# A hybrid attention and linear-attention encoder layer: the pace at which side work is dealt out between the matmuls of the projections

## Chip, cores and metric

The kernel runs on one core of one Trainium2 chip. The metric is the time of one execution on the device in microseconds (us); lower is better. Engines are named as in the profile: PE (TensorE matmuls), PEld (its weight loads), DVE (VectorE), ACT (ScalarE), POOL (GpSimd) and SP (SyncE, which here only issues DMAs).

## What is computed

One encoder layer over 512 tokens of width 2048, in float32:

```
h = rmsnorm(x, attn_norm_w); proj = h @ w_in
aq, ak, av, gq, gk, gv, gr, glr = split(proj)
attn = mixture_of_dilations(aq, ak, av, rel_bias_table)    # 16 heads x 64, softmax over a banded, biased score matrix
log_a = log_sigmoid(glr @ gla_gate_w + gla_gate_b) / 16    # one for each direction
o = gla(gq, gk, gv, log_a_fwd) + flipped gla(..., log_a_bwd)   # 4 heads, dk 128, dv 256, a gated linear recurrence
gla_out = rmsnorm_per_head(o) * gla_norm_w * silu(gr)
x = x + concat(attn, gla_out) @ w_out
h = rmsnorm(x, ffn_norm_w)
x = x + (silu(h @ w_gate) * (h @ w_up)) @ w_down           # hidden width 5632
out = rmsnorm(x, final_norm_w)
```

## The kernel before

Each float32 operand of a large product is split into a rounded part ("hi", made by ACT) and a rest ("lo", made by DVE as operand minus hi), and a product is three matmuls: hi·hi, hi·lo, lo·hi (lines 337 to 339 and 346 to 348). Nearly all the time is a long row of such matmuls. The order of instructions on every engine is written out by hand; each engine runs its own list in that order and waits on semaphores.

**Jobs and halves.** `run_job` (from line 305) runs one block of 512 output columns. A job has 16 (or 8) "halves"; one half is one 128-row slice of the weights, multiplied into four PSUM banks, three matmuls of 512 columns to a bank. The order of the jobs that matter here is: q and k of linear attention for two heads (gqk0), its v (gv0), then gqk1 and gv1, 16 halves each; then the first halves of three column blocks of `w_out`, which need only attention's result (o1, o2, o3: 8 halves each); column block 0 of `w_out` whole (out0: 16 halves); the rest of blocks 1 to 3 (c1, c2, c3: 8 halves each); then gate and up (`ff.run`) and down. Weights come by `st.load` (an SP DMA, line 209), are rounded some halves ahead (ACT, line 237) and get their rest from DVE (line 218).

**Side work.** Attention and linear attention are Python generators whose turns are dealt out between matmuls by credit. For jobs with `fine = True` (gqk0 to gv1 and o1 to o3) a quarter of the job's `rate` is credited after each bank, and a whole credit buys one turn; after the last bank of a half as many turns as there are whole credits. For out0 to c3 the whole rate is credited once for each half. The rates are `RATES = (2.5, 5.0)`: 2.5 turns to a half in gqk0 to gv1, 5.0 in o1 to o3; out0 to c3 have 1.0. The queue `side` holds first the low-rank gate input (14 turns), then `attention()` (70 units of two turns), then, from the end of gv0, `turns(... gla(h) ..., APART)` over the four heads of linear attention. `turns` begins a head every 12 rounds and gives a round two turns: one for each of two heads at work, or one real and one empty turn where only one is.

A unit of attention goes through scores (PE, 631 and 632), maximum (DVE, 641), exponential (ACT, 649), reciprocal and, for odd units, scaling (DVE 652, ACT 658), transposes (PE, 663), rounding (ACT, 671), rest (DVE, 677) and the product with v (PE, 687 and 688), each a turn or two after the one before. A head of linear attention has 22 stages, among them the gate input (PE 924, ACT 934 to 936, DVE 937), prefix sums (DVE 946, 952), centring (DVE 964 to 967), exponentials (ACT 974 to 976), products (DVE 983), the masked score blocks and transposes (PE 1015 and 1018, DVE 1021, ACT 1025), state sums (PE 1040, ACT 1049), the chain of states (DVE 1059), the output product (PE 1087), its norm, and transposes (PE 1111, DVE 1114).

**Other queues.** `urgent` is a second queue; `run_urgent` gives its first generator one turn. It is called at the start of every `run_side`, and by `before_out` at the start of each half of c1 to c3. It carries `load_qk` (operands of the next pair of heads), `gates()` (silu of the output gate times linear attention's output, then hi and lo of that: the operands of halves 8 to 15 of out0) and `rest()` of each output block (squares, transposes, and the operands of gate and up). `gates()` is queued at the norm stage of the last head. A third generator, `ff.ahead()` (DVE additions at line 1478), sums blocks of gate weights in advance; `j.ahead` of its turns are credited for each half. It has 21 blocks of four additions and needs 85 turns.

`before_out(c)` also loads the first gate and up blocks by `ff.load` (SP, line 1390), forms their sums by `ff.sums` (DVE, 1409 to 1411, twice a call) and splits them by `ff.split` (ACT 1422, DVE 1427). It counts halves through c2 and c3: `i` is 0 to 7 in c2, 8 to 15 in c3.

**Banks and slots.** The eight PSUM banks, and the tiles ("slots") in two pools, are handed out first freed, first used. At the end of a job its four banks are emptied by DVE (836, 839 after gqk; 1297 after o1 to c3) or ACT (862 after gv).

Of the kernel before, what the change touches and what calls it, by code (L numbers as in the profile page):

```python
# [26 lines left out]
KT = D // P  # L27
# [85 lines left out]
def put(*slots):  # L113
    for s in slots:
        if s.home is not None:
            s.home.free.append(s.i)


def layer(nc, tc, x, attn_norm_w, w_in, rel_table, gw_f, gb_f, gw_b, gb_b, gla_norm_w, w_out,
# [7 lines left out]
    with tc.manual_schedule(), \  # L127
# [118 lines left out]
        def piece512(w, col, kt):  # L246

            ws = w if isinstance(w, list) else [(w, col)]
            n = 512 // len(ws)
            segs = []  # L250
            for i, (wi, c) in enumerate(ws):
                src = wi[kt * P:(kt + 2) * P, c:c + n].rearrange("(k p) c -> p k c", p=P)
                segs.append((src, lambda t, i=i, n=n: t.rearrange("p (k c) -> p k c", k=2)[:, :, i * n:(i + 1) * n]))
            return segs
# [9 lines left out]
        def run_urgent():  # L264
            while urgent:
                try:
                    next(urgent[0])
                    break
                except StopIteration:
                    urgent.popleft()  # L270
# [26 lines left out]
        def job(kind, pieces, kts, acts, evac, rate=0.0, before=None, start=None, limit=None):  # L297

            j = Job()
            j.kind, j.kts, j.acts, j.evac, j.rate, j.before, j.start, j.limit = \  # L300
                kind, kts, acts, evac, rate, before, start, limit
            j.first = len(st.halves)
            st.add(pieces)
            j.n = len(st.halves) - j.first
            jobs.append(j)
            return j
# [63 lines left out]
        def rstd_of(*a):  # L370
            for _ in rstd_parts(*a):
                pass
# [15 lines left out]
        def rows_of(rstd):  # L388

            b = ps.get()  # L390
            for t in range(4):
                mm(b.t[:, t * P:(t + 1) * P], rstd[:, t:t + 1].to_broadcast([P, P]), idn,
                   start=True, stop=True)
            s = s2.get()
            act.copy(s.t, b.t)
            put(b)
            return s

        def weighted(tiles, k, wc, f):

            b = ps.get()
            for t in range(4):
                pe.transpose(b.t[:, t * P:(t + 1) * P], tiles[t].t[:, (k % 4) * P:(k % 4 + 1) * P], idn)
            act.activation(f, b.t, AF.Copy, scale=wcol[:, wc + k:wc + k + 1])
            put(b)
# [106 lines left out]
        def squares(c, t, tiles, ss, at_=None):  # L512
            junk = s2.get()
            m = c + (4 * t if at_ is None else at_)
            act.activation(junk.t, tiles[t].t, AF.Square, accum_out=ss[:, m:m + 1])
            put(junk)
# [314 lines left out]
        def evac_gqk(pr):  # L831
            def f(banks):
                for i in range(4):
                    t = s2.get()
                    if i < 2:
                        dve.scalar_tensor_tensor(t.t, banks[i].t, P ** -0.5, rb[1].t,
                                                 op0=OP.mult, op1=OP.mult)
                    else:
                        dve.tensor_tensor(t.t, banks[i].t, rb[1].t, op=OP.mult)
                    put(banks[i])  # L840
                    pool.dma_start(out=gqd[4 * pr + i], in_=t.t)
                    put(t)
            return f
# [13 lines left out]
        def evac_gv(pr):  # L857
            def f(banks):
                for t in range(4):
                    if t % 2 == 0:  # L860
                        v = s4.get(F32, [P, 2, 512])
                    act.activation(v.t[:, t % 2], banks[t].t, AF.Copy, scale=rstd1[:, t:t + 1])
                    put(banks[t])
                    if t % 2:
                        pool.dma_start(out=gvd[2 * pr + t // 2], in_=v.t.rearrange("p b c -> p (b c)"))
                        put(v)
                if pr == 0:
                    side.append(turns(deque(gla(h) for h in range(NG)), APART))
            return f
# [349 lines left out]
                fr.late()  # L1219

        n_front = len(jobs)
        RATES = (2.5, 5.0)
        APART = 12
        for pr in range(2):
            seg = [(w_in, C_GQ + pr * 256), (w_in, C_GK + pr * 256)]
            job("A", [piece512(seg, None, k) for k in range(0, KT, 2)], list(range(KT)), acts_h,
                evac_gqk(pr), rate=RATES[0], start=gstart if pr == 0 else None,
                before=None if pr else before_first, limit=3)
            job("B", [piece512(w_in, C_GV + pr * 512, k) for k in range(0, KT, 2)], list(range(KT)), acts_h,
                evac_gv(pr), rate=RATES[0])  # L1230

# [4 lines left out]
        def free_h():  # L1236
            for k in range(KT):
                put(*hT.pop(k))
            put(rb.pop(1))
# [54 lines left out]
        def evac_out(c, part=False):  # L1294
            def f(banks):
                for t in range(4):
                    dve.tensor_tensor(x1[c][t].t, x1[c][t].t, banks[t].t, op=OP.add)
                    put(banks[t])
                if not part:
                    urgent.append(rest())  # L1300

            def rest():
                yield
                for t in range(4):
                    squares(c, t, x1[c], ss2)
                    pool.dma_start(out=xd[4 * c + t], in_=x1[c][t].t)
                if c == 3:
                    dve.tensor_reduce(sum2, ss2.rearrange("p (t c) -> p t c", c=4), op=OP.add,
                                      axis=mybir.AxisListType.X)
                    rstd_of(sum2, 4, rstd2, 1.0 / D, scr)  # L1310
                fs_ = {}
                for q in (2 * c, 2 * c + 1):
                    fs_[q] = s4.get(F32, [P, 2, 512])
                    for k in range(2):
                        weighted(x1[c], 2 * q + k, W_FFN, fs_[q].t[:, k])
                    yield
                put(*x1.pop(c))
                if c == 3:
                    rb[2] = rows_of(rstd2)
                for q in (2 * c, 2 * c + 1):  # L1320
                    yield from pair_operands(q, fs_.pop(q))
            return f

        def before_out(c):
            def f(i):
                run_urgent()
                if c >= 2:
                    i += 8 * (c - 2)
                    if i >= 6:
                        ff.most = 3 if i < 9 else 5  # L1330
                        ff.load()
                    if i in (8, 9, 11, 12, 14):
                        ff.sums(ff.n_sums, halves=True)
                    if i in (13, 15):
                        ff.split((i - 13) // 2)
            return f

        def start_out(c):
            def f():
                if c == 1:  # L1340
                    free_h()
                if c == 3:
                    load_gates()
                load_res(c)
            return f

        def drop_mix(k):
            put(*mixh.pop(k))

        def job_out(c, a, z, evac, **kw):  # L1350
            return job("B", [piece512(w_out, c * 512, k) for k in range(a, z, 2)], list(range(a, z)),
                       lambda k: mixh[k], evac, limit=3, **kw)

        for c in (1, 2, 3):
            job_out(c, 0, 8, evac_out(c, True), rate=RATES[1], start=start_out(c))
        n_in = len(jobs)
        for j in jobs[n_front:]:
            j.fine = True
        jobs[n_front + 3].lead = lambda i: AHEAD + (i > 11) + (i > 13)
        j = job_out(0, 0, KT, evac_out(0), rate=1.0, start=start_out(0))  # L1360
        j.drop = lambda k: drop_mix(k) if k < 8 else None
        for j in jobs[n_front + 4:]:
            j.lead = lambda i: AHEAD + 2
        for c in (1, 2, 3):
            j = job_out(c, 8, KT, evac_out(c), rate=1.0, before=before_out(c))
        j.drop = drop_mix

        n_out = len(jobs) - 1
# [650 lines left out]
        for c in range(4):  # L2019
            j = job("B", [piece512(w_down, c * 512, k) for k in (0, 2)], list(range(4)),  # L2020
                    lambda k: gT[k], evac_down(c), before=before_down(c))
# [6 lines left out]
        for c in range(4):  # L2028
            j = job("B", [piece512(w_down, c * 512, k) for k in (LAST - 4, LAST - 2)], list(range(LAST - 4, LAST)),
                    lambda k: gT[k], evac_later(c), before=before_later(c))  # L2030
# [96 lines left out]
        run_last = finish()  # L2127
        state["sums"] = ff.ahead()
        for n, j in enumerate(jobs):
            j.ahead = 2.0 if n_in <= n < n_out else 1.0 if n_in - 3 <= n < n_in else 0.0  # L2130
        for n, j in enumerate(jobs):
            if n == n_down:
                dn.run()
# [40 lines left out]
```

## Time and profile before

| | |
|---|---|
| time, median of 3 runs | 2173.07 us (2172.14 to 2173.58) |
| the profiled execution | 2172.39 us, span 2170.6 us |
| PE, PEld, DVE, ACT busy | 99%, 87%, 84%, 56% |
| matmuls | 12682 |
| bytes moved | 405.71 MB, 187 GB/s |
| granted TensorE clock | 0.999 |

The profile names an instruction by engine, line, and output and input tile. "Idle before" is the time that an engine waited just before an instruction, with what ended the wait. A matmul's row lasts longer than the matmul holds PE, since matmuls are pipelined: the distance from one start to the next is what it costs.

### The profile page before, as it was taken

The numbers are of one execution on the slowest core, as the hardware profiler recorded it, in microseconds if no ns is written. First come the engines' busy times: TensorE is split into PE (matmuls) and PEld (weight loads), VectorE is DVE, ScalarE is ACT, GpSimd is POOL, SyncE is SP. The second block draws the span as 40 slices with busy tenths as digits, with TensorE's granted clock in tenths as the row PEclk, the third lists the DMA queues.
The fourth block names the chain that finished last, engine by engine and source line by source line (L and its number), as shares of the span: only waits on it lengthen the run. The fifth ranks groups of instructions, "written<-read, shape, count | busy, mean of one in ns | idle before, by whom it ended". The sixth has DMA issues, their size and how long they took to land.

```text
span 2170.6 us, 34926 instructions
## 1 busy us (share of the span) xinstructions
PE 2151.7 (99%) x12682; PEld 1898.7 (87%) x12682; DVE 1824.4 (84%) x3161; ACT 1221.2 (56%) x2228; POOL 358.0 (16%) x499
## 2 busy tenths in 40 slices
PE   9999999999999999999999999999999999999998
PEld 7888887888877888888888888888888899999987
DVE  6689996777778769899899898998989888898885
ACT  8455555677655546455555555555555655555562
POOL 0012213111021110021221112211221120021300
PEclk9999999999999999999999999999999999999999
DMA  6467779445365684477766677676776985576982
GB/s 202 138 177 183 178 183 250 151 139 174 123 224 175 235 278 137 136 182 182 187 178 182 181 180 196 173 184 178 177 199 176 267 205 174 180 182 156 289 304 78
DMA packets 264411, 405.71 MB, mean 187 GB/s; under 512 B 19309, under 2 KB 163357, under 8 KB 264238
## 3 DMA queue, kind: packets, MB, share of 16 engines
q1 hardware_dynamic: 205502, 272.49, 39.3%
q0 software_dynamic: 58416, 130.45, 26.4%
q8 instruction: 100, 1.64, 0.3%
q14 instruction: 73, 0.60, 0.1%
q10 hardware_dynamic: 320, 0.53, 0.1%
HBM read 287.47 MB, written 66.39 MB: 163 GB/s over the span
## 4 chain that ended last, share of the span: by engine, by line
PE 58%; DVE 0%; DMA 0%; issue 0%; ACT 0%; DVEq 0%; ACTq 0%
PE ps L1518 24%; PE ps L1504 12%; PE ps L1877 5%; PE ps L1876 5%; PE ps L1875 5%; PE ps L347 1%; PE ps L346 1%; PE ps L348 1%; PE ps L2072 1%; PE ps L2070 1%; PE ps L2071 1%; DMA gd<-b 0%; DVE b L1427 0%; DVE a L2103 0%; DVE a L1538 0%
## 5 line engine op out<-in xcount | busy, mean ns | idle before, releaser
L1422 ACT CAST b<-b 128x768 fp32r<-128x768 f32 (+1 forms) x569 | 518.9, 944 | 370.4 <-DVE b L1427 172.8
L1427 DVE TENSOR_TENSOR b<-b,b 128x768 fp32r<-128x768 f32 (+1 forms) x569 | 597.0, 1084 | 29.8 <-ACT b L1422 18.5
L1518 PE MATMUL ps<-b,b 128*128 128x512 f32 x1656 | 484.1, 393 | 0.4 <-ACT b L1422 0.2
L1518 PE MATMUL ps<-a,b 128*128 128x512 f32 x1368 | 401.0, 394 | 0.2 <-DVE b L1538 0.2
L1518 PEld LDWEIGHTS ps<-b,b 128*128 128x128 f32 x1656 | 280.8, 188 | 31.9 <-ACT b L1422 0.6
L1504 PEld LDWEIGHTS ps<-b,b 128*128 128x128 f32 x1656 | 271.4, 190 | 39.2
L1504 PE MATMUL ps<-b,b 128*128 128x256 f32 x1656 | 296.8, 280 | 0.0
L1504 PEld LDWEIGHTS ps<-a,b 128*128 128x128 f32 x1368 | 227.3, 189 | 36.7 <-DVE b L1427 0.5
L1518 PEld LDWEIGHTS ps<-a,b 128*128 128x128 f32 x1368 | 228.1, 189 | 22.7 <-issue 0.6
L1504 PE MATMUL ps<-a,b 128*128 128x256 f32 x1368 | 245.6, 280 | 0.1
L1409 DVE TENSOR_TENSOR b<-b 128x512 f32<-128x512 f32 x260 | 177.9, 684 | 17.4 <-DMA b<-in_w_down_dram 7.2
L1875 PE MATMUL ps<-b,b 128*128 128x256 f32 x624 | 176.6, 283 | 0.0
L1876 PE MATMUL ps<-b,b 128*128 128x256 f32 x624 | 176.6, 283 | 0.0
L1877 PE MATMUL ps<-b,b 128*128 128x256 f32 x624 | 176.6, 283 | 0.0
L1875 PEld LDWEIGHTS ps<-b,b 128*128 128x128 f32 x624 | 119.8, 192 | 0.0
L1876 PEld LDWEIGHTS ps<-b,b 128*128 128x128 f32 x624 | 119.8, 192 | 0.0
L1877 PEld LDWEIGHTS ps<-b,b 128*128 128x128 f32 x624 | 119.8, 192 | 0.0
L346 PE MATMUL ps<-b,b 128*128 128x512 f32 x296 | 119.0, 402 | 0.0
L1410 DVE TENSOR_TENSOR b<-b,b 128x256 f32<-128x256 f32 x260 | 110.6, 425 | 9.0
L1411 DVE TENSOR_TENSOR b<-b,b 128x256 f32<-128x256 f32 x260 | 110.6, 425 | 8.9
L347 PE MATMUL ps<-b,b 128*128 128x512 f32 x296 | 115.6, 391 | 0.0
L348 PE MATMUL ps<-b,b 128*128 128x512 f32 x296 | 115.6, 391 | 0.0
(301 smaller groups left out, 4190.3 us busy)
## 6 DMA issues: line engine op xcount, KB each, us to landing
b<-in_w_gate_dram SPq DMA_DIRECT2D x109, 512.0 KB, 3.7
b<-in_w_up_dram SPq DMA_DIRECT2D x88, 512.0 KB, 3.8
b<-in_w_down_dram SPq DMA_DIRECT2D x88, 512.0 KB, 5.5
b<-a POOLq DMA_DIRECT2D x162, 256.0 KB, 4.4
b<-in_w_in_dram SPq DMA_DIRECT2D x78, 512.0 KB, 3.8
b<-in_w_out_dram SPq DMA_DIRECT2D x32, 512.0 KB, 6.9
gd<-b POOLq DMA_DIRECT2D x22, 512.0 KB, 4.0
b<-gd SPq DMA_DIRECT2D x22, 512.0 KB, 5.8
```

Of the source, the lines that this page charges most:

```text
L346: mm(o, xh.t[:, c], wh.t[:, w], start=first and not on, stop=False, skip_group_check=on)
L347: mm(o, xh.t[:, c], wl.t[:, w], start=False, stop=False, skip_group_check=on)
L348: mm(o, xl.t[:, c], wh.t[:, w], start=False, stop=last, skip_group_check=on)
L1409: dve.tensor_tensor(s_[:, :, 0:2], r[:, :, 1:3], r[:, :, 0:1].to_broadcast(shape), op=OP.add)
L1410: dve.tensor_tensor(s_[:, :, 2], s_[:, :, 0], r[:, :, 2], op=OP.add)
L1422: act.copy(o, src)
L1427: dve.tensor_tensor(o, src, h, op=OP.subtract)
L1504: mm(o, wl, xh, start=False, stop=end, skip_group_check=True)
L1518: mm(o.rearrange("p (s t) -> p s t", s=2), wh, x_, start=first and p == 0, stop=False, skip_group_check=True)
L1875: mm(o, xh[:, t], wh, start=first and h == 0, stop=False, skip_group_check=True)
L1876: mm(o, xh[:, t], wl, start=False, stop=False, skip_group_check=True)
L1877: mm(o, xl[:, t], wh, start=False, stop=last, skip_group_check=True)
```

## The change

Five things are changed in the order of work; no arithmetic is added or taken away.

```diff
-        RATES = (2.5, 5.0)
+        RATES = (2.8, 3.75)
```

Side turns in gqk0 to gv1 go from 2.5 to 2.8 a half, those in o1 to o3 from 5.0 to 3.75.

```diff
         def before_out(c):
             def f(i):
-                run_urgent()
+                if c or i < 8:
+                    run_urgent()
                 if c >= 2:
                     i += 8 * (c - 2)
-                    if i >= 6:
+                    if i >= 3:
                         ff.most = 3 if i < 9 else 5
                         ff.load()
-                    if i in (8, 9, 11, 12, 14):
+                    if i in (5, 7, 9, 11, 13):
                         ff.sums(ff.n_sums, halves=True)
                     if i in (13, 15):
                         ff.split((i - 13) // 2)
...
-        j = job_out(0, 0, KT, evac_out(0), rate=1.0, start=start_out(0))
+        j = job_out(0, 0, KT, evac_out(0), rate=1.0, start=start_out(0), before=before_out(0))
```

Halves 0 to 7 of out0 give the urgent queue one turn more each. The first loads of gate weights come three halves earlier, and two of the five calls of `ff.sums` move from c3 to c2.

```diff
         for n, j in enumerate(jobs):
-            j.ahead = 2.0 if n_in <= n < n_out else 1.0 if n_in - 3 <= n < n_in else 0.0
+            j.ahead = {n_out: 0.0, n_out - 1: 1.0}.get(n, 2.0 if n_in <= n < n_out else 1.25 if n_in - 3 <= n < n_in else 0.0)
```

The sums in advance get 1.25 turns a half in o1 to o3 (1.0 before), 2.0 in out0 and c1 as before, 1.0 in c2 (2.0 before), none in c3 as before.

## Prediction, made before the changed kernel was run

> **What bounds the kernel now.** I read the page first, then the waits of PE, then windows around the stages that the change touches.
>
> ```profile
> PE 2151.7 (99%) x12682; PEld 1898.7 (87%) x12682; DVE 1824.4 (84%) x3161; ACT 1221.2 (56%) x2228; POOL 358.0 (16%) x499
> ```
>
> ```profile
> 408.00:556.00 148.00, 147.24 (x807) 124.88 (x806) 113.49 (x267) 108.74 (x229) 24.16 (x46) 1.00 0.50 154
> 614.00:691.00 77.00, 71.87 (x360) 60.07 (x358) 62.82 (x124) 46.88 (x109) 19.07 (x36) 1.00 0.70 243
> 719.00:766.00 47.00, 47.00 (x213) 38.99 (x212) 38.23 (x81) 23.13 (x46) 5.38 (x10) 1.00 0.84 287
> 820.00:847.00 27.00, 25.33 (x124) 20.77 (x123) 25.27 (x65) 14.50 (x33) 1.37 (x3) 1.00 0.50 171
> 853.00:2171.00 1318.00, 1308.83 (x8279) 1185.72 (x8277) 1158.48 (x1833) 716.66 (x1200) 219.13 (x267) 1.00 0.69 187
> ```
>
> The columns are the window, its length, the busy time of PE, PEld, DVE, ACT and POOL, PE's clock and the DMA share. The first row is dense attention (gv0, gqk1), the second linear attention (o1, o2), the third out0, the fourth c3. PE is the bound everywhere, at full clock. The edits reorder work and leave every matmul in place, so the time can move only by PE's waits from about 335 us, where side work begins, to 853 us, where gate and up run. After 853 us PE is dense again, so what is won or lost before it arrives whole at the end. The waits of PE in this stretch, as total, times and longest:
>
> ```profile
> PE ps L1087 <- DVE b L1297: 2.3, 1, 2.3
> PE ps L1015 <- DVE a L983: 2.0, 1, 2.0
> PE ps L1087 <- DVE b L1059: 1.7, 2, 1.1
> PE ps L347 <- DVE a L218: 1.7, 2, 1.0
> PE ps L631 <- DVE b L677: 0.8, 1, 0.8
> PE ps L339 <- DVE a L218: 0.3, 1, 0.3
> ```
>
> They sum to 8.8 us, 0.4% of the time. This is the whole prize, and the price is paid in new waits. 0.2% (4.3 us) is about what a measurement of this kernel can tell from no change.
>
> ```profile
> 621.20 0.39 PE L348 MATMUL ps<-a,a 128*128 128x512 f32 x1
> 623.58 0.60 PE L1015 MATMUL ps<-a,a 128*128 128x128 f32 x3 [1.99 <-DVE a L983]
> ...
> 689.16 0.39 PE L348 MATMUL ps<-b,a 128*128 128x512 f32 x1
> 691.83 1.13 PE L1087 MATMUL ps<-b,a 128*128 128x256 f32 x4 [2.29 <-DVE b L1297]
> ```
>
> A wait costs slightly more than its row: from 621.20 to 623.58 are 2.38 us where unhindered matmuls start about 0.23 apart (417.48 and 417.71, below), so 2.15 us are lost, 0.16 more than the 1.99 named. Three such bank rows make 0.68 us; I count distances in banks of 0.68 us, four to a half.
>
> **Where the turns fall.** A 16-half job deals out 15.75 times its rate. Low-rank (14 turns) and attention (140) need 154. At 2.5 that is 61.6 of the 63 credited halves, at 2.8 only 55. So linear attention now begins in half 9 of gv1, where one head alone gets a real turn every 2/2.8 = 0.71 halves. By the end of gv1 22 turns of it are spent (3.5 before), by the end of o1 22.4 + 29.1 = 51.5 (42.2 before), by the end of o2 80.5 (81 before): the boundary from o2 to o3 meets the same stages as before. About 8 turns remain for out0.
>
> **First wait of linear attention (L1015, 2.0 us).** It lies in o1, where between the first prefix sum and L1015 only 9 banks (6.1 us) of matmuls lie. DVE must do there two of each of these, four products (L983), and weight rests:
>
> ```profile
> 687.18 1.23 DVE L952 TENSOR_TENSOR_SCAN a<-a,a 128x512 f32<-128x512 f32 x1
> 688.32 1.05 DVE L1059 SCALAR_TENSOR_TENSOR b<-b,small 128x256 f32<-128x256 f32 x2
> ...
> 690.16 0.68 DVE L946 TENSOR_TENSOR a<-a,a 128x512 f32<-128x512 f32 x1
> 690.76 0.41 DVE L1478 TENSOR_TENSOR b<-b 128x256 f32<-128x256 f32 x1
> 691.10 0.68 DVE L1297 TENSOR_TENSOR b<-b,ps 128x512 f32<-128x512 f32 x1
> ```
>
> Scans and subtractions are 2 × (1.23 + 0.68) = 3.8 us, the products 4 × 0.68 = 2.7, two centrings of about 1 us each and two weight rests of 0.68: 9.9 us, so PE waits. After the change 17 banks (11.6 us) lie there, with no L1478 beside it. The wait goes: -2.0 us (between -2.0 and 0).
>
> **Output products behind the chain of states (L1087 on L1059, 1.7 us, heads 0 and 1).** From the gate stage of the next head to L1087 are 4 banks for head 0 and 5 for head 1. After: 6 and 8, but for head 1 the emptying of o1's banks (four L1297, 2.7 us) falls in between. I take 1.7 to 0.5: -1.2 us (-1.7 to 0).
>
> **Output product at the end of o2 (2.3 us, head 2).** The same stages meet this boundary. DVE works without a gap up to 691.10, and the emptied bank that L1087 takes is free at 691.78. From the next head's gate input to L1087 are 11 banks where there were 9, a gain of 1.36 us, less about one L1478 more (0.41). So 2.3 to 1.3: -1.0 us (-2.3 to 0).
>
> **A new wait at the end of o1.** There all eight banks are taken (four by o1, two by head 2's gate input, two by head 1's state sums), and the next state sums, one bank into o2, take the bank that o1's fourth L1297 frees. DVE can begin the last of four 0.68 us additions only when that bank's matmuls end; queued behind head 2's L937 and three additions it ends about 1.4 us into o2, where PE asks after 0.68: +0.7 us. Bounds: 0, and 2.3 us as at the o2 boundary now. Behind the waiting matmul stands all of PE.
>
> **Attention at 2.8.** A turn now follows after 4/2.8 = 1.43 banks instead of 1.6, so 0.17 × 0.68 = 0.12 us sooner, and the five turns from scores to transposes give the chain over DVE and ACT 0.6 us less. What slack is there? ACT's scaling and the transposes that need it, once tight, once usual:
>
> ```profile
> 417.04 0.73 ACT L658 ACTIVATE a<-a,small 128x512 f32<-128x512 f32 x1 [0.98 <-DVE small L652]
> 437.22 0.72 ACT L658 ACTIVATE a<-a,small 128x512 f32<-128x512 f32 x1
> ```
>
> ```profile
> 417.48 0.39 PE L347 MATMUL ps<-a,b 128*128 128x512 f32 x1
> 417.71 0.39 PE L348 MATMUL ps<-a,b 128*128 128x512 f32 x1
> 417.94 0.60 PE L663 MATMUL ps<-idn,a 128*128 128x128 f32 x4
> ...
> 439.20 0.49 PE L663 MATMUL ps<-idn,a 128*128 128x128 f32 x3
> ```
>
> Scaling ended at 417.77, 0.17 us before PE came; the other time at 437.94, 1.26 us before. A unit as tight as the first pays 0.6 - 0.17 = 0.43 us, one like the second nothing. There are 32 odd units; I take three as tight as the first, near the boundaries of jobs and the operands of a new pair: +1.2 us (0, since PE hardly waits now, to 32 × 0.43 = 13.8). It is nearer to the low end because DVE (113 of 148 us) and ACT (109 of 148) have room. Emptying gqk0 now falls at unit 15, not at unit 12 where a pair's result is merged and PE waited 0.8 us: to 0.3, -0.5 us (-0.8 to +0.5). The early 0.3 us at L339 stays.
>
> **out0.** The last head's norm and transposes, and all of `gates()`, move into it. With two urgent turns a half DVE has about two products and two rests (2.7 us), a weight rest (0.68) and two L1478 (0.8): 4.2 us against 2.73 of matmuls, some 9 us behind after six halves. The cover is what DVE has free in out0 now, 47 - 38.23 = 8.8 us, and the wait at its end:
>
> ```profile
> DVE b L1297 <- PE ps L348: 8.8, 2, 7.3
> ```
>
> The rest for half 8 is queued three halves (8.2 us) ahead, later ones more. Cost 0; without the cover up to 1.5 us a half.
>
> **c2 and c3.** A call of `ff.sums` is two each of L1409, L1410 and L1411:
>
> ```profile
> L1409 DVE TENSOR_TENSOR a<-b 128x256 f32<-128x256 f32 x14 | 5.8, 418 | 0.0
> L1411 DVE TENSOR_TENSOR a<-a,b 128x128 f32<-128x128 f32 x14 | 4.1, 292 | 0.5
> L1410 DVE TENSOR_TENSOR a<-a,b 128x128 f32<-128x128 f32 x14 | 4.1, 292 | 0.5
> ```
>
> That is 2 × (0.42 + 0.29 + 0.29) = 2.0 us. c2 gains two calls (4.0) and loses eight L1478 (3.3), so it stays as it is. c3 loses 4.0 us, and its PE waits are 1.7 us:
>
> ```profile
> 826.19 0.69 DVE L218 TENSOR_TENSOR a<-b,a 128x512 fp32r<-128x512 f32 x1 [0.94 <-ACT a L237]
> ...
> 842.24 0.68 DVE L218 TENSOR_TENSOR a<-b,a 128x512 fp32r<-128x512 f32 x1
> ```
>
> But DVE sits idle until 826.19 for ACT, and from there to the last weight rest at 842.24 the calls number two before (halves 3 and 4) and two after (3 and 5). The call saved at half 0 lies ahead of the idle time and only lengthens it. So the first of the two waits goes and the last grows as much: 0 (-1.7 to 0). SP loads three gate blocks earlier, ahead of the last `w_out` pieces:
>
> ```profile
> 818.47 0.38 SPq L209 DMA_DIRECT2D b<-in_w_out_dram  x1
> ```
>
> ```profile
> 838.13 0.61 ACT L237 CAST a<-b 128x512 fp32r<-128x512 f32 x1
> ```
>
> The last piece is read 19.7 us after its issue, which covers that. POOL's fetches for the first head only come earlier.
>
> **The sum.** -2.0 - 1.2 - 1.0 + 0.7 + 1.2 - 0.5 + 0 = -2.8; three waits vanish with 0.16 us each on top: -3.3 us. The profiled execution takes 2172.39 us, its span 2170.6; it would take 2169.1. The median of the runs is 0.68 us above the profiled one, so 2169.8 us.
>
> By the Trainium skill, page "Trainium Kernel Development and Optimization", section Performance Expectations, the busy share of weight loads tells more than that of matmuls. By that rule the second window (60.07 of 77) brought to the first's share (124.88 of 148) would shrink by 5.8 us, an estimate, to 2167.3 us.
>
> **Rivals.** *All of it goes.* The 8.5 us without L339 vanish, with six times 0.16, and only the new 0.7 is paid: -8.8, 2164.3 us. For it: DVE's room. Against: ACT gates c3, and the o2 boundary meets the same stages.
>
> *The waits only move.* The first goes (-2.0), and head 0 and 1 gain 1.2, but the o2 boundary keeps its 2.3, the new one costs 2.3 too, attention 2.5, L631 loses 0.5, vanished rows 0.3: +0.8, 2173.9 us. For it: banks are handed out in turn, so boundaries stay places to wait.
>
> *Attention becomes bound by its chain.* If all 32 odd units are as tight as the one at 417.94, attention costs 13.8 us instead of 1.2: +9.3, 2182.4 us. It decides from about 9 us, 21 tight units, where the sum passes +0.2%. Against it: the usual slack of 1.26 us. By the Trainium skill, page "TensorE: Matmul & The Clock Gate", part 1, an idle window of about 3.4 us halves the clock; the rows show 1.00 throughout and no wait above 2.3 us.
>
> **How the numbers follow.** The forecast gets 0.45 (its own range 2167.0 to 2172.0, a little over a third of it below 2168.7, the 0.2% line), all of it 0.23, moved waits 0.18, bound attention 0.14. Faster 0.17 + 0.23 = 0.40; within 0.2% 0.28 + 0.18 = 0.46; slower 0.14. The range from 2164.0 to 2175.5 leaves out bound attention and the far part of the second case.
>
> **What would show it.** Among PE's waits L1015 on L983 is gone and L1087 on L1059 is under 0.8; L1087 on L1297 is there at the start of o3, near 1.3, and L1040 or L1087 waits on L1297 at the start of o2; L347 on L218 is still there at the end of c3; L663 waits on ACT L658 for 1 to 2 us in all. Wrong would be a wait on L658 or L677 above 5 us, one of L347 in out0 on the operands of `gates()`, or a wait on a `w_out` DMA.

## The result, and the profile after

The changed kernel takes 2186.41 us (median of 6 runs, 2184.95 to 2189.13), the kernel before beside it 2173.23 us (2172.14 to 2174.47): a ratio of 1.0062, 95% interval 1.0049 to 1.0075. It is slower by 13.2 us where 3.3 us less were forecast. The profiled executions are 2186.63 us (span 2184.9) and 2172.39 us (span 2170.6), 14.2 us apart. The busy times of the engines on the page are those of before, but for PE, whose 5.5 us more are not work (12682 matmuls as before):

```profile
PE 2157.2 (99%) x12682; PEld 1898.0 (87%) x12682; DVE 1825.4 (84%) x3161; ACT 1221.1 (56%) x2228; POOL 357.0 (16%) x499
```

The waits of PE in the changed kernel (total, times, longest):

```profile
PE ps L631 <- DVE b L677: 4.4, 5, 1.3
PE ps L1040 <- ACT b L1049: 3.9, 1, 3.9
PE ps L347 <- DVE a L218: 2.0, 1, 2.0
PE ps L1087 <- DVE b L1297: 1.7, 1, 1.7
PE ps L663 <- ACT a L658: 1.7, 4, 0.5
PE ps L631 <- DVE a L836: 1.1, 2, 0.6
...
PE ps L346 <- DVE b L677: 0.7, 1, 0.7
...
PE ps L1040 <- DVE b L1297: 0.3, 1, 0.3
```

L1015 on L983 and L1087 on L1059 are gone. New are the scores of attention (L631) waiting for the rests of DVE (L677), 4.4 us where there were 0.8, and a wait of 3.9 us for ACT's scaling of linear attention's states (L1049). These rows grew by far less than 13 us, so I worked out the loss of each stage from the starts of all its matmuls: the distance from one start to the next, less what it is where nothing hinders (0.227 us for 512 columns, less for narrower ones), in us:

| | before | after |
|---|---|---|
| gqk0 to gv1 (attention) | 3.8 | 15.1 |
| o1, o2, o3 | 6.3, 6.1, 8.1 | 9.7, 4.6, 7.2 |
| out0, c1, c2 | 0 | 0 |
| c3 | 2.3 | 2.3 |

(The three o jobs hold several us in every version: linear attention's matmuls of 256 columns, L1040 and L1087, start 0.215 us apart where attention's, L687 and L688, start 0.12 apart. The differences between versions are what counts.) Attention costs 11.3 us more. o1 costs 3.4 more, which o2 and o3 give back but for 1.0. The rest is 1.2 us in gate and up and 0.6 before attention. Two places are to be explained: attention, and the wait in o1.

**Attention.** A window over dense attention in the changed kernel (length, then PE, PEld, DVE, ACT, POOL busy, clock, DMA share):

```profile
411.00:569.00 158.00, 152.01 (x824) 125.31 (x825) 118.98 (x284) 112.20 (x238) 24.12 (x46) 1.00 0.48 143
```

PE now stands idle for 6.0 us, where it was 0.8 in the window of before, and neither DVE (75% busy) nor ACT (71%) is full. What are these two doing in the rest of the time? First the kernel before, then the changed one, both from 335 to 610 us:

```profile
DVE b L677 <- ACT b L671: 46.3, 48, 2.5
ACT a L658 <- DVE small L652: 29.3, 25, 2.4
...
ACT a L649 <- DVE small L641: 24.7, 29, 1.4
```

```profile
DVE b L677 <- ACT b L671: 46.3, 50, 2.2
...
ACT a L658 <- DVE small L652: 31.0, 25, 2.3
ACT a L649 <- DVE small L641: 30.1, 29, 2.4
```

They wait for each other. DVE's rest waits for ACT's rounding, ACT's exponential waits for DVE's maximum, some 50 and 30 times. ACT's scaling also waits for DVE's reciprocal (L658 on L652). All three rows stand in the trace of before, and they are hardly larger after the change, so the totals alone don't show what these waits cost PE; the experiments below do. One round of it in the changed kernel, on DVE, then ACT, then PE:

```profile
521.87 0.69 DVE L677 TENSOR_TENSOR b<-ps,b 128x512 fp32r<-128x512 f32 x1 [1.10 <-ACT b L671]
522.48 0.68 DVE L641 CUSTOM_DVE_ANT_0 a<-ps,b 128x512 f32<-128x512 f32 x1
...
523.80 1.41 DVE L588 SCALAR_TENSOR_TENSOR a<-a,a 64x512 fp32r<-64x512 f32 x2
525.13 0.68 DVE L218 TENSOR_TENSOR a<-b,a 128x512 fp32r<-128x512 f32 x1
525.85 0.69 DVE L588 SCALAR_TENSOR_TENSOR a<-a,a 64x512 fp32r<-64x512 f32 x1
526.57 0.69 DVE L677 TENSOR_TENSOR b<-ps,b 128x512 fp32r<-128x512 f32 x1
```

```profile
523.20 0.73 ACT L649 ACTIVATE a<-a,small 128x512 f32<-128x512 f32 x1 [0.31 <-DVE small L641]
523.83 0.18 ACT L649 ACTIVATION_READ_ACCUMULATOR a<-a,small 128x1 f32 x1
523.92 0.57 ACT L671 CAST b<-ps 128x512 fp32r<-128x512 f32 x1
```

```profile
525.58 0.40 PE L339 MATMUL ps<-b,a 128*128 128x512 f32 x1
527.31 0.50 PE L631 MATMUL ps<-a,a 128*128 128x512 f32 x1 [1.33 <-DVE b L677]
```

The maximum is queued on DVE behind the rest of an older unit. The exponential waits for the maximum. The rounding of the older unit, whose transposes have long been there, is queued on ACT behind the exponential, and the next rest needs that rounding. So a unit can't be shorter than this ring: from the rest at 521.87 to the end of the rounding at 524.49 are 2.6 us. What else is queued inside it comes on top. Here that is L588 and L218: DVE works without a gap from 521.87 until the next rest at 526.57, which therefore finds its rounding done, and the 1.10 us that DVE stood still before 521.87 are not made up. The scores, which need the bank that this rest empties, come late by 1.33 us. From first to last scores the units took 3.58 us each before ((589.00 - 363.48) / 63). At 2.8 PE would give them two turns of 0.12 us less, 3.34, and got 3.52 ((584.50 - 362.64) / 63).

**o1.** On POOL, ACT and PE:

```profile
628.36 0.54 POOL L865 DMA_DIRECT2D gvd<-b  x1 [2.18 <-ACT b L862]
```

```profile
635.54 1.20 ACT L1049 ACTIVATE b<-ps,small 128x256 f32<-128x256 f32 x3 [5.97 <-DMA gvd<-b]
```

```profile
632.14 0.40 PE L348 MATMUL ps<-a,a 128*128 128x512 f32 x1
636.43 2.93 PE L1040 MATMUL ps<-b,a 128*128 128x256 f32 x6 [3.90 <-ACT b L1049]
638.80 0.99 PE L346 MATMUL ps<-a,a 128*128 128x512 f32 x1
```

ACT writes the first states of head 0 into a slot of `s4`, and the slot that is next in turn is the one from which gv1's last block is still being stored to DRAM. The store was issued at 628.36 and let go 7.2 us later. PE's next state sums need the bank that ACT has not emptied. Before the change the store was issued at 613.77 and the first states were scaled at 630.93, 17 us later; now ACT comes to them 1.2 us after it. The wait has a second price, the clock, in the windows that follow:

```profile
632.00:636.00 4.00, 0.54 (x3) 0.09 (x1) 0.00 (x0) 0.46 (x2) 0.25 (x1) 1.00 1.01 387
636.00:640.00 4.00, 3.56 (x9) 2.89 (x10) 2.56 (x5) 3.92 (x10) 0.00 (x0) 0.57 1.04 393
```

The granted clock is 0.57 in the mean of the second window: it is at half from 636.43 to 639.84 us. By the starts of the matmuls the wait costs 4.1 us and the slow ones behind it 2.2, 6.3 us in all.

### The profile page after: what moved, and what is told of

It reads as the page before. It is cut to its first block, busy times and chain, and to the rows that moved or that the text cites. A ratio compares the mean times of both kernels' runs of the same rounds, so it can differ in the third digit from the quotient of the medians.

```text
span 2184.9 us, 34951 instructions
## 1 busy us (share of the span) xinstructions
PE 2157.2 (99%) x12682; PEld 1898.0 (87%) x12682; DVE 1825.4 (84%) x3161; ACT 1221.1 (56%) x2228; POOL 357.0 (16%) x499
## 4 chain that ended last, share of the span: by engine, by line
PE 57%; DVE 1%; DMA 0%; issue 0%; ACT 0%; DVEq 0%; ACTq 0%
PE ps L1519 24%; PE ps L1505 12%; PE ps L1878 5%; PE ps L1877 5%; PE ps L1876 5%; PE ps L347 1%; PE ps L346 1%; PE ps L348 1%; PE ps L2073 1%; PE ps L2072 1%; PE ps L2071 1%; DVE b L1428 0%; DMA gd<-b 0%; DVE a L1539 0%; DVE b L1410 0%
## 5 line engine op out<-in xcount | busy, mean ns | idle before, releaser
L347 PE MATMUL ps<-b,b 128*128 128x512 f32 x300 | 117.0, 390 | 0.0
```

Of the source, the lines that this page charges most:

```text
L347: mm(o, xh.t[:, c], wl.t[:, w], start=False, stop=False, skip_group_check=on)
```

## Experiments

Theory: two causes, each removable by one line. In attention the ring over DVE and ACT; in o1 the slot. Rivals: DVE or ACT simply have too much to do at 2.8; the scaling (L658) is late, as the prediction's fourth rival had it; the other edits cost the time; the store in o1 is slow because the DMA engines are full. The first four kernels ran beside the kernel before at 2174.23 us (2172.34 to 2177.06), the last four at 2173.99 us (2172.37 to 2177.78).

**Density alone.** Edit to the kernel before:

```diff
-        RATES = (2.5, 5.0)
+        RATES = (2.8, 5.0)
```

> The kernel before with RATES (2.8, 5.0) and nothing else of the change. If denser attention is what costs (loop theory: DVE's rest waits for ACT's rounding, which is queued behind an exponential that waits for DVE's maximum, one round trip to a unit), gqk0 to gv1 lose about 11 us of PE as in the changed kernel, where their excess over unhindered matmul starts was 15.1 us against 3.8, and linear attention gains what it gains from an early start: 2178 to 2188 us. If the loss comes from sparser steps in o1 to o3 or from the work moved into out0, it stays within 3 us of 2173.

Measured 2190.03 us, ratio 1.0071 (1.0057 to 1.0084), 2 us above the expected range. Attention loses 15.2 us, job by job what the changed kernel loses, and its waits are the same. So the rate alone does it, and the other edits have no part in it. o1 to o3 lose 26.5 (changed kernel 21.5), most of the surplus in o1 (16.6), where the chain of states comes late:

```profile
PE ps L1087 <- DVE b L1059: 5.7, 4, 3.5
```

The rate of 5.0 is not the only cause there. The same store of gv1 is in the way, now of a weight's rounding, and the next head's gate input (L934) is queued behind that on ACT; from 640.39 to 647.21 us the granted clock is 0.50. How o1's loss divides among these is not shown.

```profile
635.06 0.62 ACT L237 CAST b<-b 128x512 fp32r<-128x512 f32 x1 [3.84 <-DMA gvd<-b]
635.58 0.68 ACT L934 ACTIVATE a<-ps,wcol 128x512 f32<-128x512 f32 x1
```

**All but the rates.** Edit to the changed kernel:

```diff
-        RATES = (2.8, 3.75)
+        RATES = (2.5, 5.0)
```

> The changed kernel with the old RATES (2.5, 5.0): only the urgent turns in out0, the earlier loads and sums of gate weights, and the sums in advance are changed. Both theories: within 1.5 us of 2173.2, with the waits of linear attention (L1015, L1087) back and the wait of the last weight rest in c3 about 2 us. If the operands made sooner matter by themselves, it is below 2171.

Measured 2176.91 us, ratio 1.0012 (1.0003 to 1.0021): 2.7 us slower than before, not within 1.5 as expected. Attention loses 4.2, as before the change. The waits L1015 on L983 (2.0) and L1087 on L1059 (1.7) are back, so it was the rates that removed them. The surplus is in o3 and c3. The wait at the end of o2 has grown, and the clock falls behind it:

```profile
PE ps L1087 <- DVE b L1297: 2.7, 1, 2.7
```

```profile
694.00:698.00 4.00, 4.00 (x13) 3.21 (x12) 3.72 (x8) 0.95 (x4) 0.82 (x2) 0.57 0.31 110
```

In c3 the last weight rest comes 2.0 us late, as in the changed kernel, but here the clock is at 0.50 behind it too, from 847.60 to 851.01 us. By the starts of the matmuls these two stretches cost about 1.8 and 1.1 us, which is the whole surplus (an estimate from this one execution).

**Another slot in o1.** At the end of `free_h()`, after `put(rb.pop(1))`, the last 16 of the free slots are moved to the front, ahead of the one that the store still reads. Edit to the changed kernel:

```diff
             put(rb.pop(1))
+            s4.free.rotate(16)
```

> The changed kernel, but when the operands of the input projection are freed at the start of o1 their 16 slots are put to the front of the free list, so that the first state tile of linear attention does not get the slot from which gv1's result is still being stored. If ACT's wait for that store (5.97 us) is a wait for the slot, PE's 3.9 us wait at L1040 and the half clock behind it go, together 6.3 us by the starts of matmuls: 2179 to 2181 us. If it is the load of v or the DMA engines as such, the time stays at 2186.

Measured 2180.60 us, ratio 1.0028 (1.0017 to 1.0039), 0.34% less than the changed kernel. The wait is gone, and the windows in its place are full at full clock, though the DMA engines are as busy as they were. So it was the slot; the rival of full DMA engines falls.

```profile
632.00:636.00 4.00, 4.00 (x19) 3.36 (x18) 3.05 (x7) 3.90 (x9) 0.00 (x0) 1.00 1.04 403
636.00:640.00 4.00, 4.00 (x20) 3.40 (x19) 3.90 (x9) 0.88 (x3) 0.00 (x0) 1.00 1.02 385
```

**Rounding ahead of the exponential.** The two ACT operations change places in a turn of `attention()`; the work stays. Edit to the changed kernel:

```diff
                 run(att_scale, u - 2)
-                run(att_exp, u - 1)
                 run(att_round, u - 3)
+                run(att_exp, u - 1)
```

> The changed kernel with one swap in the attention: ACT's rounding of unit u-3 is queued ahead of the exponential of unit u-1, not behind it. Loop theory: DVE's rest then no longer waits behind the maximum of a later unit, PE's waits for L677 (4.4 and 0.7 us) and most of attention's 11 us go: 2175 to 2180 us. Rival (slack: transposes come too soon after scaling by ACT L658, whatever stands between): the swap makes the exponential and the scaling later, waits on L658 grow from 1.7 us and the time is the same or longer, 2186 or more.

Measured 2177.45 us, ratio 1.0015 (1.0007 to 1.0024), 0.47% less than the changed kernel. Attention's loss falls from 15.1 to 5.9 us. By the order of the program the rounding now stands behind the exponential of one unit earlier, so that the ring runs over two units. The mutual waits and PE's wait for the rest, from 335 to 610 us:

```profile
ACT a L658 <- DVE small L652: 29.6, 24, 1.9
...
DVE b L677 <- ACT b L671: 24.1, 31, 1.9
...
ACT a L649 <- DVE small L641: 3.8, 6, 1.7
...
PE ps L631 <- DVE b L677: 0.6, 1, 0.6
```

A window over dense attention:

```profile
409.00:560.00 151.00, 149.63 (x823) 125.98 (x823) 119.90 (x286) 112.31 (x237) 24.01 (x46) 1.00 0.51 150
```

DVE and ACT do the same work in less time, 79% and 74% busy, and PE hardly waits for them: they did not have too much to do, they were in each other's way. PE has no wait on L658 left either; the scaling was late because it, too, was in that queue. That rival falls as a cause of its own. ACT's own wait for the reciprocal (29.6 us) stays, and PE does not pay for it. Of the 11.3 us that attention lost by the change 9.2 are gone; what makes up the other 2.1 is not shown.

**The same order in the kernel before.** The swap alone, at 2.5.

> The kernel before with the swap alone (rounding ahead of the exponential). Loop theory: at 2.5 turns the loop hardly set the pace (gqk0 to gv1 had 3.8 us of excess), so only about 1 to 2 us are to be won: 0.3 to 2 us below the kernel before. If the swap helps by something else than the loop (ACT's order as such), it gains here what it gained in the changed kernel, 9 to 10 us.

Measured 2173.99 us, ratio 1.0000 (0.9992 to 1.0009). The mutual waits fall as far as at 2.8:

```profile
DVE b L677 <- ACT b L671: 26.5, 36, 2.8
...
ACT a L649 <- DVE small L641: 2.3, 2, 1.4
```

but attention's loss is 4.2 us (3.8 before): at 2.5 the ring was just hidden, and there was nothing to win, less than the 0.3 us at the low end of what I expected.

**Both, in the changed kernel.** The swap and the slots together.

> The changed kernel with the swap and with the 16 slots put first. If the two causes are separate and are the whole loss, the gains add: 13.2 us of loss less 9.6 (attention's stages in the run with the swap) less 6 (o1 in the run with the slots) leaves 2 to 3 us below the kernel before, which is near what was predicted for the change. If they are one cause seen twice, it stays 3 or more us above.

Measured 2170.51 us, ratio 0.9984 (0.9976 to 0.9993). Against the changed kernel that is 0.78% less, and the single effects sum to 0.81%: the two causes stand side by side, and together they are the whole loss and more. Attention loses 5.4 us, the o jobs 15.7 (20.5 before), c3 3.4. c3's 1.1 us more than in the changed kernel are the clock: the same late weight rest (1.9 us) is followed here by 3.4 us at half clock.

**c3's sums.** What is left of c3 was put down to where the calls of `ff.sums` fall. Edit on top of the last kernel:

```diff
-                    if i in (5, 7, 9, 11, 13):
+                    if i in (5, 7, 8, 11, 14):
```

> As the run before it, with the five calls of the gate weights' sums at halves 5, 7, 8, 11, 14 in place of 5, 7, 9, 11, 13. By the reading of c3 in the prediction (a call ahead of DVE's idle time at half 1 costs nothing, one behind it delays the last weight rest) one call fewer lies behind it, and the 2.0 us wait at L347 in c3 goes: 2 us below the run before it. If that wait is only the load of splits and evictions, it stays.

Measured 2167.94 us, ratio 0.9974 (0.9964 to 0.9984). L347 on L218 is gone, and the half clock behind it too; c3 loses 0.3 us. The calls in c3 now come at halves 0, 3 and 6 instead of 1, 3 and 5. Between DVE's wait for ACT and its last weight rest lay two of them (at 827.79 and 834.72 us in the sixth kernel); now it is one (at 828.62), the third comes behind that rest, and the rest is in time. That is the stretch that the prediction counted calls in.

**Denser still.** On top of it:

```diff
-        RATES = (2.8, 3.75)
+        RATES = (3.0, 3.4)
```

> As the run before it, with RATES (3.0, 3.4). If the loop through ACT and DVE was the only limit of attention's pace, gqk0 to gv1 keep an excess near 6 us and the time stays within 2 us of the run before it. If attention at 2.8 with the swap is already near the limit of its engines (DVE 120 and ACT 112 of 151 us), the excess grows by 5 us or more and the time with it.

Measured 2165.72 us, ratio 0.9961 (0.9949 to 0.9974), the best of the versions run and ahead of both kernels, and 2.2 us below the run before it. gqk0 to gv1 lose 7.5 us, more than the 6 expected but far from 5 more; gv1 now holds matmuls of linear attention (L1040 and L1087), whose slower steps are counted in that. The o jobs lose 11.1, c3 0.3. No wait on L1087, L1040 or L677 is left; from 335 to 853 us there are only

```profile
PE ps L339 <- DVE a L218: 1.0, 1, 1.0
PE ps L663 <- DVE a L839: 0.4, 1, 0.4
```

## Why the prediction was wrong

**The step that failed: "Attention at 2.8", +1.2 us; measured +11.3 by the starts of the matmuls.** It took three tight units of 32 because "DVE (113 of 148 us) and ACT (109 of 148) have room". That room was read from busy shares. The rows of DVE's and ACT's waits in the same trace, which the prediction does not use, say that from 335 to 610 us 46.3 and 24.7 us of their idle time were waits for each other. Such time was no room: it did not shrink when the rate grew (46.3 and 30.1 us in the changed kernel). The Trainium skill, page "Perfetto Trace Analysis", section Identifying the Most-Contended Engine, calls the occupancy of the vector and scalar engines a fair measure of how close one is to the roofline. That is not the same as room in a given order of work: at 75% and 71% they could not go faster in this order, and the swap of two instructions brought them to 79% and 74%.

The prediction's *attention becomes bound by its chain* had the sign and nearly the size (+9.3 in all), and was given 0.14. Its place was wrong: it priced the transposes' wait for the scaling, which is 1.7 us in four waits, inside the 1 to 2 us that the prediction named as right. The list of what would prove it wrong held the true place, "L658 or L677 above 5 us": on L677 wait 4.4 and 0.7 us, 5.1 in all.

**The step that was missing: a slot.** "A new wait at the end of o1" looked for one among the eight banks and found +0.7; that one is there, with 0.3. But linear attention begun earlier also takes its slots earlier, and one was still in use by a store: 6.3 us with the clock. The sentence that the clock is out of reach, with "no wait above 2.3 us", argued from the waits of before, not from those that a moved stage can make; and a wait of 2.3 us, even of 1.9, can already halve it, as the last section shows.

**What held, by its steps.** The first wait of linear attention went whole, as said. Output products behind the chain of states: forecast 0.5, measured none. The end of o2: forecast 1.3, measured 1.7. c3: "the first goes and the last grows as much": one wait of 2.0 where two made 1.7, loss unchanged at 2.3. out0 at no cost, no wait on a `w_out` DMA. (The window called out0 begins in o3, whose banks are emptied until 734 us; from 729 to 773 us DVE has 8.85 us free, hardly other than the 8.8 of the prediction. The rival *all of it goes* counts six vanished rows where the list has seven, 0.2 us.) The emptying of gqk0 was forecast to fall from 0.8 to 0.3; in the changed kernel L631 waits 0.5 us there on L836, and gv0's first matmul 0.7 on L677. With both causes removed the kernel takes 2170.51 us beside the 2169.8 forecast: attention's loss is 1.6 us above that of before (forecast +1.2 - 0.5), the o jobs' 4.8 below (forecast -2.0 - 1.2 - 1.0 + 0.7 and the 0.48 for vanished rows: -4.0), c3's 1.1 above (forecast 0; it is the clock). The sum of -3.3 us was about right for a kernel without the ring and the slot (-3.5 by the medians, -1.9 by the profiled executions), in part by luck: the terms are off by 0.8 to 1.1 us, with both signs.

## What to carry to other kernels

Before a rate is raised, look at what the engines that are "not the bound" wait for: if two of them wait for each other, add up one round of that ring, with what is queued inside it, and compare that with the new pace, rather than go by their busy shares. In an in-order queue put the operation whose input is ready ahead of the one that waits for the other engine; here that one swap was worth 0.47% at the higher rate and nothing at the lower. When a stage is moved forward, check each slot that it takes for a store still reading from it.

## What the runs showed of the hardware

A wait of 3.9 us on PE was followed by a mean granted clock of 0.57 in the next 4 us, which is a stretch of 3.41 us at half clock. Unexpected was that shorter waits can do it: 2.7 and 2.0 us in the second experiment, 2.3 us in the fifth, 1.9 us in the sixth. Yet the 2.3 us wait of the kernel before, the very same, left the clock alone, and so did the 2.0 us wait in c3 of the changed kernel.

The traces show what decides. Within one execution the changes of the clock lie whole multiples of 3.413 us apart: in the changed kernel it rises at 4.96 us and falls at 636.43, 185 of them later; in the second experiment it falls at 694.00 and again at 847.60, 45 later. So I divided the traces into windows on that grid. First two windows of the fifth experiment, then the two that hold the same wait in the kernel before:

```profile
688.15:691.56 3.41, 1.20 (x6) 0.66 (x4) 3.27 (x10) 1.25 (x3) 0.00 (x0) 1.00 0.85 310
691.56:694.98 3.42, 3.35 (x8) 2.72 (x9) 3.42 (x6) 0.00 (x0) 0.00 (x0) 0.50 0.03 13
```

```profile
689.94:693.35 3.41, 1.52 (x7) 1.37 (x8) 3.41 (x7) 1.24 (x3) 0.00 (x0) 1.00 0.40 148
693.35:696.77 3.42, 3.42 (x18) 2.97 (x17) 3.11 (x7) 1.21 (x5) 0.86 (x2) 1.00 0.00 0
```

In the fifth experiment nearly the whole wait lies in one window: PE is idle for 2.21 us of it, and the next window runs at half clock. In the kernel before a boundary at 689.94 splits the wait: 1.89 us of it lie in the window shown, and the clock stays. Over all ten executions the clock fell seven times between the first and the last matmul, each time behind a window with PE idle for 1.90 us or more (1.90, 1.95, 2.2, 2.5, 2.7, 3.3 and 3.4); no window with 1.89 or less cost anything, and two with 1.90 did not, so the border lies at about 1.9 of 3.41 us. Where the grid falls differs from run to run, and with it the price of a wait of about 2 to 3 us beyond the wait itself: nothing, or 1.1 to 1.8 us by the starts of the matmuls in these runs.

The Trainium skill, page "TensorE: Matmul & The Clock Gate", Part 1, gives a window of about 3.4 us that runs freely, so that its phase against the kernel varies; the measured 3.413 us agrees with it. That 1.9 idle us of such a window are enough is not what the page's rule, a whole idle window, says.
